# Delta rule heads in two overlapping lanes, one merge gate column behind each head, 14 merge gate columns ahead of the attention

## The chip, the cores and the metric

The kernel runs on one core of one Trainium2 chip. The metric is the device time of one execution in microseconds (us), median of several runs. A profile of one execution stands beside it: for every engine the instructions with their start and duration, what they waited for, and the clock that was granted to TensorE. PE is TensorE, DVE is VectorE, ACT is ScalarE, POOL is GpSimd, SP is SyncE, which issues the DMAs.

## The reference

One layer of a hybrid encoder for 512 prompt tokens and 8 x 16 decode tokens, 640 rows in all, in float32. Cut to what matters here:

```python
z = x @ w_in                     # 640 x 2048 by 2048 x 12312
q_a, k_a, v_a, f_a, gate_a, qkv_b, a_b, beta_b, gate_b, m_a, m_b = jnp.split(z, SPLIT_IDX, axis=-1)
# branch A: forgetting attention, 8 heads of 128
y_a = (o_a * jax.nn.silu(gate_a)) @ w_out_fox
# branch B: causal conv of width 4 on q|k|v, silu, l2 norm of q and k, then per head in chunks
u = solve(amat, vc * bc[..., None])
w = solve(amat, kb * jnp.exp(gc)[..., None])
def step(s, xs):
    v_new = u_n - w_n @ s
    o = q_n @ s + qk_n @ v_new
    s = s * gl_n + kt_n.T @ v_new
y_b = (rms_norm(o_b, gdn_norm_w) * jax.nn.silu(gate_b)) @ w_out_gdn
# merge: m_a and m_b are 2048 columns of z each, the merge gates
h = (jax.nn.sigmoid(m_a) * y_a + jax.nn.sigmoid(m_b) * y_b) @ w_out
# then layer norm, a gate projection and the per-layer embedding
```

## The kernel before

All large products are cut into **columns**: 128 output channels, 16 k-steps of 128 input channels, all 640 rows in two halves of 320. Each operand is split into a high and a low fp32r part, and three products are summed, so a k-step is six matmuls of 320 (`mm6`, L218 and L219) and a column is 96. There are 146 columns of weights, and TensorE works through them in a fixed order.

Weights come as half columns of 512 KB (`wr`, three buffers, issued by SyncE), and are split in pieces of 128 x 512 by ScalarE (`wh`, L167) and VectorE (`wl`, L168), up to six pieces ahead of their use (a column uses four).

The order around the columns is written out in Python. Each k-step ends with `tick()`, which lets each **lane** (a queue of generators) take one step when its time has come. What a generator issues between two `yield`s lands on the engines' queues at that k-step; `yield n` means n k-steps later. All engines take their instructions in the order written. So the small products of the heads stand between column matmuls, at places that the counts of `yield` set.

Stages: attention (`phase_fox`, 8 heads of q, k and gate columns, with the values' columns, L259, after the first q and k), the embedding's projection, the delta rule (`phase_gdn`), then the two output projections and the gate (`tail`). Merge gate columns (`mcol`) fill the stages in between: 3 behind the attention, 3 behind each of the delta rule's heads 0 to 6, 8 behind head 7.

A delta rule head is four columns (q, k, v and the output gate). After each of the first three, ScalarE writes the result to `strip` (L584), and the lane `conv` runs the convolution on VectorE: a first tap (L599) and three more (L603), a tanh on ScalarE, then L610 and L615. The lane `work` runs `gdn` and behind it `gdn_pro` and `gdn_dec`:

- transposes and squares (L630 to L645), norms and coefficients `cs` on VectorE (L664 to L676), transposed values (L686), key and query products (L699) with `lt` and `qk` (L706, L708);
- the unit triangular blocks of `lt` go through memory into `lanes`, and 31 steps of forward substitution run on VectorE (L732, L734); the result goes to memory (`xd`, L740) and comes back as `u0` (L743), and VectorE transposes it (L835);
- `gdn_pro`: TensorE reads that transposed tile first at L844, builds the larger inverse (L852 to L873), and then goes through the four chunks: L885 (with the state S), L891, L896, then VectorE's new state (L899, L901), L905 and L906. Each of these steps stands two k-steps behind the one that it needs;
- `gdn_dec`: the same for the decode rows with 8 states `st` (L793 to L826).

The lane `ends` runs `gdn_out` (norm and gate of the head's output, L759 to L779). A head waits to start until the output of the head before last is done. All head products share the PSUM tag "s" with four banks.

Of the kernel before, what the change touches and what calls it, by code (L numbers as in the profile page):

```python
# [17 lines left out]
P = 128  # L18
DM = 2048
T = 640  # L20
NPT = 512
# [25 lines left out]
class Kernel:  # L47
# [4 lines left out]

    PIECES = 6
    LATE = 3

# [563 lines left out]
    def gdn(self, h, kq, v, sg):  # L619
        nc, cb = self.nc, self.cb  # L620
        gr = self.zt([P, T], "gr")
        nc.sync.dma_start(out=gr, in_=bcast(self.rd[8 + h], T, P))
        st = self.zt([P, 8, P], "st")
        nc.sync.dma_start(out=st, in_=self.i["st"][h])

# [21 lines left out]
        dt = self.zt([P, 5, P], "dt")  # L647
        for t in range(5):
            m = C_DP if t < 4 else C_DD
# [26 lines left out]
        nc.vector.tensor_single_scalar(cs[:, 4, :], r[:, 5:10], GDN_SCALE, op=ALU.mult)  # L676
        kt = self.zt([P, 5, P], "kt")
        vr = self.zt([P, 5, P], "vr")
        for t in range(4):
# [11 lines left out]
        lt = self.zt([P, 5, P], "lt")  # L691
        qk = self.zt([P, 5, P], "qk")
        for t0 in (0, 2, 4):
# [18 lines left out]
        for a in range(4):  # L712
# [8 lines left out]
        for src, pad in ((kq[:, 0, NPT:T], self.kpad), (qg[:, NPT:T], self.gpad)):  # L721
            for par in range(2):
                nc.gpsimd.tensor_copy(
                    out=pad.rearrange("p (j two) c -> p j two c", two=2)[:, :, par, 16 * par:16 * par + 16],
                    in_=src.rearrange("p (j two c) -> p j two c", two=2, c=16)[:, :, par, :])
        yield 5
        x = self.zt([80, 8, 32], "sx", 2)
        tmp = self.zt([80, 8, 32], "sx2")
# [15 lines left out]
        yield 8  # L744
        uu = self.uu
        dd = [slice(32 * a, 32 * a + 32) for a in range(4)]
        for a in range(4):
            nc.gpsimd.tensor_copy(out=uu[dd[a], :, dd[a]], in_=u0[dd[a], :, :])
        yield from self.par(self.gdn_pro(h, kq, lt, qk, qg, kt, vr, cs, u0),
                            self.gdn_dec(h, qk, kt, vr, cs, st))  # L750
        self.ends["gens"].append(self.gdn_out(h, self.ob, cs, sg))

    def gdn_out(self, h, ob, cs, sg):

        nc = self.nc
# [12 lines left out]
        for t in range(5):  # L768
            nc.scalar.mul(ob[:, t, :], ob[:, t, :], f[:, t:t + 1])
        yield (30 if h < 7 else 3)  # L770
        og = self.zt([P, T], "og")
        po = self.sps()
        for t in range(4):
            nc.tensor.transpose(po[:, t * P:(t + 1) * P], ob[:, t, :], self.ident)
        nc.vector.scalar_tensor_tensor(out=og[:, 0:NPT], in0=po, scalar=self.nw, in1=sg[:, 0:NPT],
                                       op0=ALU.mult, op1=ALU.mult)
        po = self.sps()
        nc.tensor.transpose(po[:, 0:P], ob[:, 4, :], self.ident)
        nc.vector.scalar_tensor_tensor(out=og[:, NPT:T], in0=po[:, 0:P], scalar=self.nw, in1=sg[:, NPT:T],  # L779
                                       op0=ALU.mult, op1=ALU.mult)  # L780
        yield 2
        nc.sync.dma_start(out=self.ogd[8 + h], in_=og)
        self.gdone = h
        yield

    def gdn_dec(self, h, qk, kt, vr, cs, st):

        nc, cb = self.nc, self.cb
        self.ob = ob = self.zt([P, 5, P], "ob")
        pd = self.sps()  # L790
        for par in range(2):
# [11 lines left out]

        vm = self.zt([P, 2, P], "dt", 1, "vm")
        nc.gpsimd.tensor_tensor(out=vm, in0=vn[:, None, :].to_broadcast([P, 2, P]),
# [25 lines left out]
    def gdn_pro(self, h, kq, lt, qk, qg, kt, vr, cs, u0):  # L831
# [10 lines left out]
        for t in range(4):  # L842
            for a in (0, 64):
                nc.tensor.matmul(px[a + 32:a + 64, 32 * t:32 * t + 32], lt[a:a + 32, t, a + 32:a + 64],  # L844
                                 m0[a:a + 32, t, :], start=True, stop=True)
        xx = self.zt([P, 4, 32], "xx")
        for a in (32, 96):
# [18 lines left out]
        for t in range(4):  # L866
            nc.tensor.matmul(px[64:128, t * 64:(t + 1) * 64], lt[0:64, t, 64:128], t1[:, t, :], start=True, stop=True)
        x2 = self.zt([P, 4, 64], "x2")
        nc.scalar.copy(out=x2[64:128].rearrange("p a b -> p (a b)"), in_=px[64:128, 0:256])
# [44 lines left out]
    def run(self, ctx):  # L914
# [31 lines left out]
    def phase_fox(self, work):  # L946
# [71 lines left out]
        for h in range(H):  # L1018
# [3 lines left out]
            for c in range(3):  # L1022
# [51 lines left out]
    def phase_gdn(self, conv, work):  # L1074
# [7 lines left out]
        for x in (self.uu, self.t1, self.kpad, self.gpad):  # L1082
            nc.gpsimd.memset(x, 0.0)
        self.gdone = -1
        for h in range(H):
            self.until(lambda: self.gdone >= h - 2)
            kq = self.zt([P, 2, T], "kq", 2)
            v, sg = self.zt([P, T], "v"), self.zt([P, T], "sg", 2)
            for c in range(4):
                acc = self.column()[0]  # L1090
                self.until(lambda: not conv["gens"])
                if c == 3:
                    self.silu_evac(acc, sg, "cth")
                else:
                    ct = 8 * c + h
                    stp = self.strip_evac(acc, ct)
                    conv["gens"].append(self.conv_silu(stp, ct, (kq[:, 1, :], kq[:, 0, :], v)[c]))
# [315 lines left out]
def _layout(a):  # L1413
# [13 lines left out]
          for g in range(2)]  # L1427
    bl += [bq[0], bk[0], *bv[0], *bv[1], bg[0]]
    for h in range(1, H):
        bl += [bq[h], bk[h], bg[h]]  # L1430
    bl += m[:3]
    pj = _wblock(a["w_pl_proj"][0])
    pj = [pj[8 * i:8 * i + 8].transpose(1, 0, 2).reshape(P, DM) for i in range(2)]
    bl += [pj[0], pj[1]]
    for h in range(H):
        bl += [gq[h], gk[h], gv[h], gg[h]]
        if h < 7:
            bl += m[3 + 3 * h:6 + 3 * h]
    bl += m[24:]
    bl += list(_wblock(np.concatenate([a["w_out_fox"][0], a["w_out_gdn"][0]], 0)))  # L1440
# [68 lines left out]
```

## Time and profile before

| | |
|---|---|
| median of 3 runs | 2295.9 us (2295.38 to 2296.25) |
| profiled execution, its own time | 2294.97 us |
| its span, first to last instruction | 2293.1 us |
| mean granted TensorE clock | 0.999 |
| TensorE busy | 2285.8 us |
| VectorE busy | 1178.1 us |
| ScalarE busy | 727.7 us |
| HBM | 237.70 MB read, 40.67 MB written |

Matmuls are pipelined and their ends are modelled, so a busy TensorE says only that it had work in flight; how fast it goes is read from the starts of matmuls that follow each other. Rows of the order of time read: start, duration, engine, line, operation, written tile <- read tiles, shapes, count, and in brackets the idle time ahead and what ended it. A stage row reads: stretch, its length, then each engine's busy time with its count of instructions, the TensorE clock, the DMA share and GB/s.

### The profile page before, as it was taken

The numbers are of one execution on the slowest core, as the hardware profiler recorded it, in microseconds if no ns is written. First come the engines' busy times: TensorE is split into PE (matmuls) and PEld (weight loads), VectorE is DVE, ScalarE is ACT, GpSimd is POOL, SyncE is SP. The second block draws the span as 40 slices with busy tenths as digits, with TensorE's granted clock in tenths as the row PEclk, the third lists the DMA queues.
The fourth block names the chain that finished last, engine by engine and source line by source line (L and its number), as shares of the span: only waits on it lengthen the run. The fifth ranks groups of instructions, "written<-read, shape, count | busy, mean of one in ns | idle before, by whom it ended". The sixth has DMA issues, their size and how long they took to land.

```text
span 2293.1 us, 39837 instructions
## 1 busy us (share of the span) xinstructions
PE 2285.8 (100%) x16274; PEld 2202.9 (96%) x16274; DVE 1178.1 (51%) x2589; ACT 727.7 (32%) x1656; POOL 68.4 (3%) x230
## 2 busy tenths in 40 slices
PE   9999999999999999999999999999999999999999
PEld 7889999999999999999999999999999999999998
DVE  5224334433546565656565656554433533657555
ACT  4222223332523434242434242424111311333222
POOL 0000000000000000000000000000000000020000
PEclk9999999999999999999999999999999999999999
DMA  6345455444522322323232323235433322223331
GB/s 225 123 151 214 157 172 170 165 163 138 187 97 91 98 93 98 100 89 107 81 107 81 107 81 107 82 113 194 139 126 126 115 97 97 97 97 114 120 120 59
DMA packets 107431, 280.96 MB, mean 123 GB/s; under 512 B 21464, under 2 KB 28712, under 8 KB 107248
## 3 DMA queue, kind: packets, MB, share of 16 engines
q1 hardware_dynamic: 107248, 278.41, 36.2%
q8 instruction: 128, 2.10, 0.4%
q14 instruction: 55, 0.45, 0.1%
HBM read 237.70 MB, written 40.67 MB: 121 GB/s over the span
## 4 chain that ended last, share of the span: by engine, by line
PE 99%; DMA 0%; DVE 0%; SPq 0%; ACT 0%; issue 0%
PE g L218 43%; PE g L219 42%; PE g L259 4%; PE o L259 1%; PE s L511 1%; PE o L562 1%; PE s L471 1%; PE s L699 1%; PE s L821 0%; PE s L557 0%; PE s L906 0%; PE s L891 0%; PE s L896 0%; DMA wr<-in_w 0%; PE s L905 0%; PE s L885 0%
## 5 line engine op out<-in xcount | busy, mean ns | idle before, releaser
L168 DVE TENSOR_TENSOR wl<-wr,wh 128x512 fp32r<-128x512 f32 x584 | 400.4, 690 | 700.3 <-ACT wh L167 699.4
L218 PE MATMUL g<-xh,wh 128*128 128x320 f32 (+1 forms) x2160 | 694.7, 322 | 0.0
L218 PE MATMUL g<-xl,wh 128*128 128x320 f32 (+1 forms) x2160 | 668.5, 310 | 0.5 <-DVE xl L193 0.5
L219 PE MATMUL g<-xh,wh 128*128 128x320 f32 x2160 | 668.4, 309 | 0.0
L219 PE MATMUL g<-xl,wh 128*128 128x320 f32 x2160 | 668.2, 309 | 0.0
L219 PE MATMUL g<-xh,wl 128*128 128x320 f32 x2160 | 667.6, 309 | 0.0
L218 PE MATMUL g<-xh,wl 128*128 128x320 f32 (+1 forms) x2160 | 667.4, 309 | 0.0
L167 ACT CAST wh<-wr 128x512 fp32r<-128x512 f32 x584 | 361.0, 622 | 897.3 <-PE g L219 770.9
L218 PEld LDWEIGHTS g<-xh,wh 128*128 128x128 f32 x2160 | 407.1, 188 | 15.9 <-issue 13.4
L219 PEld LDWEIGHTS g<-xh,wh 128*128 128x128 f32 x2160 | 407.5, 189 | 0.8
L218 PEld LDWEIGHTS g<-xl,wh 128*128 128x128 f32 x2160 | 407.1, 188 | 1.0 <-DVE xl L193 1.0
L219 PEld LDWEIGHTS g<-xl,wh 128*128 128x128 f32 x2160 | 407.1, 188 | 0.0
L219 PEld LDWEIGHTS g<-xh,wl 128*128 128x128 f32 x2160 | 406.4, 188 | 0.0
L218 PEld LDWEIGHTS g<-xh,wl 128*128 128x128 f32 x2160 | 406.1, 188 | 0.1
L734 DVE TENSOR_TENSOR sx<-sx,sx 80x240 f32<-80x240 f32 (+14 forms) x240 | 68.2, 284 | 8.2
L732 DVE TENSOR_TENSOR sx<-sx,lanes 80x240 f32<-80x240 f32 (+14 forms) x240 | 68.2, 284 | 7.4
L603 DVE SCALAR_TENSOR_TENSOR cy<-strip,taps,cy 128x664 f32<-128x664 f32 x72 | 65.4, 909 | 2.1
L1224 DVE SCALAR_TENSOR_TENSOR sab<-sab,g 128x320 f32<-128x320 f32 x64 | 28.4, 485 | 69.4 <-PE g L218 64.2
L259 PE MATMUL g<-wh,xh 128*128 128x512 f32 x128 | 50.7, 396 | 0.0
L259 PE MATMUL g<-wl,xh 128*128 128x512 f32 x128 | 50.6, 395 | 0.0
L259 PE MATMUL g<-wh,xl 128*128 128x512 f32 x128 | 50.5, 394 | 0.0
L1070 ACT ACTIVATE m<-g 128x320 f32<-128x320 f32 x64 | 24.5, 435 | 67.5 <-PE g L218 67.5
(338 smaller groups left out, 1840.5 us busy)
## 6 DMA issues: line engine op xcount, KB each, us to landing
wr<-in_w SPq DMA_DIRECT2D x290, 512.0 KB
kc<-in_kc SPq DMA_DIRECT2D x32, 512.0 KB
vc<-in_vc SPq DMA_DIRECT2D x32, 512.0 KB
xr<-in_xT SPq DMA_DIRECT2D x32, 320.0 KB
md<-m SPq DMA_DIRECT2D x32, 320.0 KB
sab<-md SPq DMA_DIRECT2D x32, 320.0 KB
ogd<-og SPq DMA_DIRECT2D x16, 320.0 KB
ed<-e SPq DMA_DIRECT2D x16, 320.0 KB
```

The source lines that it names most:

```text
L167: nc.scalar.copy(out=hi, in_=src)
L168: nc.vector.tensor_tensor(out=lo, in0=src, in1=hi.bitcast(F32), op=ALU.subtract)
L218: nc.tensor.matmul(ps[0], whl[w], xhl[o][:, a], start=(first and x == 0), stop=(last and x == 2))
L219: nc.tensor.matmul(ps[1], whl[w], xhl[o][:, b], start=(first and x == 0), stop=(last and x == 2))
L259: nc.tensor.matmul(ps, x[:, sl], w, start=(s == 0 and n == 0), stop=(s == 15 and n == 2))
L471: nc.tensor.matmul(s1[32 * j:32 * j + 32, :], self.qpad[:, 2 * j + par, :], kc[:, (j % 2) * NPT:(j % 2 + 1) * NPT], start=(par == 0), stop ...
L511: nc.tensor.matmul(od[32 * j:32 * j + 32, 0:P], self.ppad[:, c, 2 * j + par, :], vc[:, o:o + P], start=False, stop=(par == 1 and c == 3), ...
L603: nc.vector.scalar_tensor_tensor(out=y[:, 0:CV], in0=strip[:, i:i + CV], scalar=tp[:, 4 * ct + i:4 * ct + i + 1], in1=y[:, 0:CV], op0=ALU. ...
L732: nc.vector.tensor_tensor(out=tmp[:, :, 0:n], in0=xo[:, :, j:j + 1].to_broadcast([80, 8, n]), in1=lanes[:, j:j + 1, j + 1:32].to_broadcast ...
L734: nc.vector.tensor_tensor(out=x[:, :, j + 1:32], in0=xo[:, :, j + 1:32], in1=tmp[:, :, 0:n], op=ALU.subtract)
L1070: nc.scalar.activation(m[:, hf * HALF:(hf + 1) * HALF], acc[hf], AF.Tanh, scale=0.5)
L1224: nc.vector.scalar_tensor_tensor(out=x[:, sl], in0=x[:, sl], scalar=1.0, in1=ps[hf], op0=ALU.add, op1=ALU.mult)
```

## The change

A head of the delta rule is cut in two. `gdn` ends when `u0` has been asked for, and hands the rest to a new generator, `gdn_chunks`, in a lane of its own (`self.chunks`). So the first part of head h + 1 runs beside the chunks of head h. Tiles that both need get second buffers (gr, kt, vr, qk), others share or lose one (lanes, sx, m0, sx2); the load of `st` and the padded copies move to the start of `gdn_chunks`, `gdn_dec` starts six k-steps later, and `gdn_out` waits 10 k-steps instead of 30 ahead of its transposes.

Gate columns: 14 stand behind the first q and k columns (`FRONT`), ahead of the values; 3 behind the attention as before; one (`FILL`) behind each of heads 0 to 6; 8 behind head 7 as before. The weights are laid out in the new order.

```diff
+    FRONT = 32 - 11 - 7
+    FILL = 1
@@ gdn
-        gr = self.zt([P, T], "gr")
+        gr = self.zt([P, T], "gr", 2)
-        st = self.zt([P, 8, P], "st")
-        nc.sync.dma_start(out=st, in_=self.i["st"][h])
-        kt = self.zt([P, 5, P], "kt")
-        vr = self.zt([P, 5, P], "vr")
+        kt = self.zt([P, 5, P], "kt", 2)
+        vr = self.zt([P, 5, P], "vr", 2)
-        qk = self.zt([P, 5, P], "qk")
+        qk = self.zt([P, 5, P], "qk", 2)
-        lanes = self.zt([80, 32, 32], "lv", 1, "lanes")
+        lanes = self.zt([80, 32, 32], "hl", 1, "lanes")
-        x = self.zt([80, 8, 32], "sx", 2)
+        x = self.zt([80, 8, 32], "sx")
         u0 = self.zt([P, 5, 32], "u0")
         nc.sync.dma_start(out=u0, in_=bass.AP(self.xd.tensor, self.xd.offset, [[32, P], [4096, 5], [1, 32]]))
         yield 8
-        uu = self.uu
+        self.chunks["gens"].append(self.gdn_chunks(h, kq, lt, qk, qg, kt, vr, cs, u0, sg))
+
+    def gdn_chunks(self, h, kq, lt, qk, qg, kt, vr, cs, u0, sg):
+        nc, uu = self.nc, self.uu
+        st = self.zt([P, 8, P], "st")
+        nc.sync.dma_start(out=st, in_=self.i["st"][h])
...
         for a in range(4):
             nc.gpsimd.tensor_copy(out=uu[dd[a], :, dd[a]], in_=u0[dd[a], :, :])
         yield from self.par(self.gdn_pro(h, kq, lt, qk, qg, kt, vr, cs, u0),
                             self.gdn_dec(h, qk, kt, vr, cs, st))
+        self.bdone = h
         self.ends["gens"].append(self.gdn_out(h, self.ob, cs, sg))
@@ gdn_out
-        yield (30 if h < 7 else 3)
-        og = self.zt([P, T], "og")
+        yield (10 if h < 7 else 3)
+        og = sg
@@ gdn_dec
         self.ob = ob = self.zt([P, 5, P], "ob")
+        yield 6
@@ run
+        self.chunks = self.lane()
@@ phase_fox
                     if h == 0:
+                        for _ in range(self.FRONT):
+                            self.mcol("sc")
                         values(0)
                         values(1)
@@ phase_gdn
         for h in range(H):
-            self.until(lambda: self.gdone >= h - 2)
-            kq = self.zt([P, 2, T], "kq", 2)
-            v, sg = self.zt([P, T], "v"), self.zt([P, T], "sg", 2)
             for c in range(4):
                 acc = self.column()[0]
+                if c == 0:
+                    self.until(lambda: self.bdone >= h - 2)
+                    kq = self.zt([P, 2, T], "kq", 2)
+                if c == 2:
+                    v = self.zt([P, T], "v")
                 self.until(lambda: not conv["gens"])
                 if c == 3:
+                    self.until(lambda: self.gdone >= h - 2)
+                    sg = self.zt([P, T], "sg", 2)
                     self.silu_evac(acc, sg, "cth")
...
-            for _ in range(3 if h < 7 else 6):
+            for _ in range(self.FILL if h < 7 else 6):
                 self.mcol("cth")
```

How this moves instructions, at the places of which the prediction speaks. Lines of the changed kernel are 2 to 8 higher than before behind the additions: L899 is the former L891, L904 L896, L909 L901, L727 and L729 the substitution's L732 and L734.

VectorE in the delta rule, the end of a head's norms, before (`cs` holds the coefficients, `wl` is a weight piece, `hl` the next split of keys and queries):

```order
L674 TENSOR_TENSOR cs<-rry,ecol 128x5
L675 TENSOR_TENSOR cs<-cs,rry 128x5
L676 TENSOR_SCALAR cs<-rry 128x5
L168 TENSOR_TENSOR wl<-wr,wh 128x512 x2
L664 TENSOR_TENSOR hl<-kq,hl 128x512
```

And now (`S` is the state of the head before, `rp` the right side of its next chunk):

```order
L674 TENSOR_TENSOR cs<-rry,ecol 128x5
L675 TENSOR_TENSOR cs<-cs,rry 128x5
L676 TENSOR_SCALAR cs<-rry 128x5
L909 SCALAR_TENSOR_TENSOR S<-S,gl,s 128x128
L895 SCALAR_TENSOR_TENSOR rp<-s,negc,vr 128x128
L170 TENSOR_TENSOR wl<-wr,wh 128x512
```

The state update of one head now stands behind the norms of the next.

TensorE at the same place now, without the column matmuls between (two k-steps lie between L899 and L904, one between L914 and L686, and one between L686 and L893):

```order
L899 MATMUL s<-rp,uu 128x128
...
L904 MATMUL s<-vn,kt 128x128
L913 MATMUL s<-S,gr 128x128
L914 MATMUL s<-vn,qk 128x128
...
L686 MATMUL s<-cb,v 128x128 x4
...
L893 MATMUL s<-S,kq 128x128
```

Before, nothing of another head stood near L686; now the transposes of one head (L686) stand between the chunk steps of the other, and L893 reads the S of the VectorE row above.

VectorE at the end of a substitution, before (`sx` is the solution, `lanes` the blocks, `m` the transposed result):

```order
L732 TENSOR_TENSOR sx_8553<-sx,lanes 80x8
L734 TENSOR_TENSOR sx<-sx,sx_8553 80x8
L168 TENSOR_TENSOR wl<-wr,wh 128x512 x4
L835 STREAM_TRANSPOSE m_8843<-u_8771 128x128
```

And now:

```order
L601 TENSOR_SCALAR cy<-strip,taps 128x664
...
L605 SCALAR_TENSOR_TENSOR cy<-strip,taps,cy 128x664
L727 TENSOR_TENSOR sx_13145<-sx,lanes 80x8
L729 TENSOR_TENSOR sx<-sx,sx_13145 80x8
L605 SCALAR_TENSOR_TENSOR cy<-strip,taps,cy 128x664
L170 TENSOR_TENSOR wl<-wr,wh 128x512
L612 SCALAR_TENSOR_TENSOR kq<-cth,cy 128x512
L617 SCALAR_TENSOR_TENSOR kq<-cth,cy 128x128
L170 TENSOR_TENSOR wl<-wr,wh 128x512 x3
L601 TENSOR_SCALAR cy<-strip,taps 128x664
L843 STREAM_TRANSPOSE m_13461<-u_13378 128x128
```

The next head's convolutions (`cy`) now stand inside the substitution and between it and the transposition; earlier in it stand L612 and L617 of the convolution before.

More of the change, by code (lines that the diff above doesn't have):

```diff
@@ L717, in gdn @@
         yield 5
-        lanes = self.zt([80, 32, 32], "lv", 1, "lanes")
+        lanes = self.zt([80, 32, 32], "hl", 1, "lanes")
         nc.sync.dma_start(out=lanes.rearrange("p j i -> p (j i)"),
                           in_=bass.AP(self.ld.tensor, self.ld.offset, [[1024, 20], [0, 4], [1, 1024]]))
[L721 to L725, printed above, removed]
         yield 5
-        x = self.zt([80, 8, 32], "sx", 2)
+        x = self.zt([80, 8, 32], "sx")
         tmp = self.zt([80, 8, 32], "sx2")
@@ L744, in gdn @@
         yield 8
-        uu = self.uu
+        self.chunks["gens"].append(self.gdn_chunks(h, kq, lt, qk, qg, kt, vr, cs, u0, sg))
[3 more added lines that the diff above has]
+        nc.sync.dma_start(out=st, in_=self.i["st"][h])
+        for src, pad in ((kq[:, 0, NPT:T], self.kpad), (qg[:, NPT:T], self.gpad)):
+            for par in range(2):
+                nc.gpsimd.tensor_copy(
+                    out=pad.rearrange("p (j two) c -> p j two c", two=2)[:, :, par, 16 * par:16 * par + 16],
+                    in_=src.rearrange("p (j two c) -> p j two c", two=2, c=16)[:, :, par, :])
         dd = [slice(32 * a, 32 * a + 32) for a in range(4)]
@@ L802, in gdn_dec @@
         nc.scalar.mul(vn, pd[:, 0:P], cs[:, 2, 4:5])
-        vm = self.zt([P, 2, P], "dt", 1, "vm")
+        vm = self.zt([P, 2, P], "vm")
         nc.gpsimd.tensor_tensor(out=vm, in0=vn[:, None, :].to_broadcast([P, 2, P]),
@@ L845, in gdn_pro @@
                                  m0[a:a + 32, t, :], start=True, stop=True)
-        xx = self.zt([P, 4, 32], "xx")
+        xx = self.zt([P, 4, 32], "m0", 1, "xx")
         for a in (32, 96):
@@ L867, in gdn_pro @@
             nc.tensor.matmul(px[64:128, t * 64:(t + 1) * 64], lt[0:64, t, 64:128], t1[:, t, :], start=True, stop=True)
-        x2 = self.zt([P, 4, 64], "x2")
+        x2 = self.zt([P, 4, 64], "sx2", 1, "x2")
         nc.scalar.copy(out=x2[64:128].rearrange("p a b -> p (a b)"), in_=px[64:128, 0:256])
@@ L1427, in _layout @@
           for g in range(2)]
-    bl += [bq[0], bk[0], *bv[0], *bv[1], bg[0]]
+    nf, r = Kernel.FRONT, Kernel.FILL
+    bl += [bq[0], bk[0], *m[:nf], *bv[0], *bv[1], bg[0]]
     for h in range(1, H):
         bl += [bq[h], bk[h], bg[h]]
-    bl += m[:3]
+    bl += m[nf:nf + 3]
     pj = _wblock(a["w_pl_proj"][0])
@@ L1437, in _layout @@
         if h < 7:
-            bl += m[3 + 3 * h:6 + 3 * h]
-    bl += m[24:]
+            bl += m[nf + 3 + r * h:nf + 3 + r * (h + 1)]
+    bl += m[nf + 3 + 7 * r:]
     bl += list(_wblock(np.concatenate([a["w_out_fox"][0], a["w_out_gdn"][0]], 0)))
```

4 lines of the change are left out of this document (2 added, 2 removed).

## The prediction

> **What bounds the kernel now.** I read the page first (busy shares, then the chain that ended last), then the engines' busy time by stage, then the spacing of single matmuls in the order of time.
>
> ```profile
> span 2293.1 us, 39837 instructions
> PE 2285.8 (100%) x16274; PEld 2202.9 (96%) x16274; DVE 1178.1 (51%) x2589; ACT 727.7 (32%) x1656; POOL 68.4 (3%) x230
> PE 99%; DMA 0%; DVE 0%; SPq 0%; ACT 0%; issue 0%
> 900.00:1100.00 200.00, 200.00 (x1506) 195.04 (x1505) 123.44 (x348) 72.94 (x206) 10.47 (x34) 1.00 0.31 99
> 1101.37 0.31 PE L218 MATMUL g<-xh,wl 128*128 128x320 f32 x1
> 1101.51 0.31 PE L219 MATMUL g<-xh,wl 128*128 128x320 f32 x1
> 1101.66 0.39 PE L891 MATMUL s<-vr,uu 128*128 128x128 f32 x2
> 1101.80 0.39 PE L218 MATMUL g<-xh,wh 128*128 128x320 f32 x1
> 1102.03 0.31 PE L219 MATMUL g<-xh,wh 128*128 128x320 f32 x1
> ```
>
> TensorE is busy for the whole span, at the full granted clock (the 1.00 in the stage row), and the chain that ended last is 99% TensorE. In the stage 900 to 1100, in the middle of the delta rule, VectorE has 123.4 of 200 us. The single rows say what a busy TensorE is here: column matmuls start 0.147 us apart, and two fp32 passes of a head (L891) put between them take 1102.03 - 1101.51 - 2 x 0.147 = 0.23 us, which is what they would take anywhere. So the kernel is a list of TensorE work with no holes. Moving work on that list cannot shorten it; it can only open holes. Where a TensorE instruction has to wait, every column matmul behind it waits too, and the end moves by as much. The question is which waits the new order makes.
>
> **The change part by part.** The columns are the same 146, and each head has the same products. What is cheap first. The 14 gate columns ahead of the values cost what they cost elsewhere. In the list of TensorE's order the groups of head work between columns fall from 351 to 338; by the rows above a break costs nothing beyond its passes, at most the 0.23 us of a small group, so the 13 are worth 0 to 3 us, and I take 1. Second buffers (gr, kt, vr, qk) free no wait that the trace shows. The state load (st) is now issued at the start of the chunks, six k-steps (5.3 us) ahead of its first reader; I take 0 for it, since the hole that I find below stands between the two, and a load that is late all the same would only lengthen that hole.
>
> The price is the cover. The seven-column heads gave 112 k-steps each (a k-step is six column matmuls, 0.88 us); five columns give 80. Two in-order engines, VectorE above all, now run two heads' steps at once at places where TensorE waits for them.
>
> *Wait B, the substitution.* The chain in a head of the kernel before (head 1):
>
> ```profile
> 829.64 0.77 ACT L1070 ACTIVATE m<-g 128x320 f32<-128x320 f32 x2 [3.10 <-PE g L218]
> 834.23 0.40 DVE L732 TENSOR_TENSOR sx<-eye,lanes 80x248 f32<-80x248 f32 x1
> 855.81 0.17 DVE L734 TENSOR_TENSOR sx<-sx,sx 80x8 f32<-80x8 f32 x1
> 856.01 0.34 SPq L740 DMA_DIRECT2D xd<-sx  x1
> 857.73 0.38 SPq L743 DMA_DIRECT2D u<-xd  x1
> 859.85 0.31 DVE L835 STREAM_TRANSPOSE m<-u 128x128 f32<-128x128 f32 x1
> 861.21 0.44 PE L844 MATMUL s<-m,lt 32*32 32x32 f32 x16
> L844 PE MATMUL s<-m,lt x128: 190/191/213, 748.5 to 1537.9; 32*32 32x32 f32 x128
> ```
>
> The substitution fills VectorE from 834.23, 4.6 us after the end of a column (829.64), to 855.98. Its result goes out and back through memory, is transposed at 860.16, and TensorE reads it at 861.21. Only 1.05 us are spare; with the signal's way I count 1.0. In the list of the changed order the reader stands as far behind the last L699 as before (258 column matmuls both times), but the lane columns of the next head are now q and k columns instead of gate columns, so VectorE gets convolutions just there:
>
> ```profile
> 878.96 0.43 ACT L584 COPY strip<-g 128x320 f32<-128x320 f32 x1
> 880.93 0.56 DVE L599 TENSOR_SCALAR cy<-strip,taps 128x664 f32<-128x664 f32 x1
> 881.67 2.79 DVE L603 SCALAR_TENSOR_TENSOR cy<-strip,taps,cy 128x664 f32<-128x664 f32 x3
> 885.35 0.69 DVE L610 SCALAR_TENSOR_TENSOR kq<-cth,cy 128x512 f32<-128x512 f32 x1
> 885.96 0.29 DVE L615 SCALAR_TENSOR_TENSOR kq<-cth,cy 128x128 f32<-128x128 f32 x1
> 821.35 0.75 DVE L775 SCALAR_TENSOR_TENSOR og<-s,cvec,sg 128x512 f32<-128x512 f32 x1 [2.02 <-PE s L774]
> 822.01 0.34 DVE L779 SCALAR_TENSOR_TENSOR og<-s,cvec,sg 128x128 f32<-128x128 f32 x1
> 855.92 1.90 DVE L168 TENSOR_TENSOR wl<-wr,wh 128x512 fp32r<-128x512 f32 x3
> ```
>
> - Ahead of the substitution: a convolution's taps end 881.67 + 2.79 - 878.96 = 5.5 us after their column; then the last head's output products (822.35 - 821.35 = 1.0) and one weight piece (1.90 / 3 = 0.6) make 7.1 instead of 4.6: +2.5 us.
> - Inside it, by the changed order: the rest of that convolution (0.9) and of the next one the first tap (0.5) and two more (2 x 0.93): +3.2 us.
> - Behind it, ahead of the transposition: one tap, a weight piece, the convolution's end after a tanh, three weight pieces and the next first tap, 0.9 + 0.6 + 0.9 + 1.9 + 0.5 = 4.8 and about 1.1 for ScalarE in between, so 5.9 instead of the 4.2 of the way through memory (855.98 to 860.16): +1.7 us.
>
> So 2.5 + 3.2 + 1.7 - 1.0 = 6.4 us of TensorE idle in a head. Bounds: 3.7 (1.5 ahead, nothing behind) and 8 (another 1.6 of ScalarE). Heads 1 to 6 have it, head 0 without the output products (5.4), head 7 has gate columns behind it and none: 6 x 6.4 + 5.4 = 44 us.
>
> *Wait A, the state behind the norms.*
>
> ```profile
> 803.56 0.73 ACT L655 ACTIVATE gr<-gr 128x640 f32<-128x640 f32 x1
> 804.70 0.62 ACT L663 CAST hl<-kq 128x512 fp32r<-128x512 f32 x1
> 804.74 0.60 PE L686 MATMUL s<-cb,v 128*128 128x128 f32 x4
> 805.44 0.68 DVE L664 TENSOR_TENSOR hl<-kq,hl 128x512 fp32r<-128x512 f32 x1
> 808.93 0.17 DVE L676 TENSOR_SCALAR cs<-rry 128x5 f32<-128x5 f32 x1
> 884.98 0.34 DVE L901 SCALAR_TENSOR_TENSOR S<-S,gl,s 128x128 f32<-128x128 f32 x1
> 801.47 0.28 ACT L645 ACTIVATE junk<-s 128x128 f32<-128x128 f32 x1 [0.23 <-PE s L643]
> ```
>
> VectorE's norms and coefficients (L664 to L676) run to 809.10, 4.36 us after TensorE has passed L686; before, nothing on TensorE waited for them. In the changed order the previous head's state update L901 stands right behind them on VectorE, and TensorE needs that state two places on (the next L885, and by a shared PSUM bank already L686): 4.36 + 0.34 = 4.7 us. TensorE gets there later, by the nine products of the other lane between (9 x 0.23 = 2.1); the norms start later too, since their last squares wait for TensorE (the 0.23 at 801.47) and ScalarE has two more instructions ahead: +1.4. That leaves 4.0 us, with bounds of 2.6 (norms not delayed) and 5. Seven heads: 28 us. The four PSUM banks also make one state product wait for a VectorE read once in a head, 0.34 and the way there: 0.5 x 7 = 3.5 us.
>
> *The clock after a wait.*
>
> ```profile
> 2288.00:2293.00 5.00, 0.00 (x0) 0.00 (x0) 1.29 (x4) 0.51 (x1) 0.00 (x0) 0.74 0.08 26
> 2287.21 0.28 PE L212 MATMUL g<-xh,wl 128*128 128x256 f32 x1
> 1.19 4.02 PE L969 MATMUL wu<-z 128*128 128x512 bf16 x9 [1.19 <-DVE z L966]
> 5.69 0.47 PE L218 MATMUL g<-xl,wh 128*128 128x320 f32 x1
> 5.95 0.47 PE L219 MATMUL g<-xl,wh 128*128 128x320 f32 x1
> 7.05 0.30 PE L219 MATMUL g<-xh,wh 128*128 128x320 f32 x1
> ```
>
> The last matmul ends at 2287.49; a mean clock of 0.74 over the next 5 us, if it goes from 1 to the 0.5 of the slow rows, puts the drop 2.9 us after it. At the start the pace is 0.267 us (5.69 to 5.95) until about 7, 5.9 us after the first matmul. A hole as long as B closes the clock, then; one costs up to 5.9 x (1 - 0.147 / 0.267) = 2.65 us, at least 0. I take 2.0, near the upper end since 6.4 is well past 2.9: 7 x 2.0 = 14 us. For A (4.0) I take none.
>
> The Trainium skill, "TensorE: Matmul & The Clock Gate", Part 1, says that the clock is halved after a whole idle window of about 3.4 us of a free-running counter. By that, as an estimate, a hole of 6.4 us holds a window 9 times in 10 and one of 4.0 about 2 times in 10, so the term would be some 7 x 2.65 x 1.1 = 20 us. The single drop at 2.9 us here is no contradiction that a trace of before can settle.
>
> **Sum**: 44 + 28 + 3.5 + 14 - 1 = 88 us. The profiled execution took 2294.97 us (span 2293.1), 0.9 below the median of the three runs; 2295 + 88 = 2383.
>
> **Rivals.**
> 1. One of the two waits never reaches TensorE. For: each rests on a few us between queues, and the norms may start earlier than I think. A alone gives 2295 + 28 + 3.5 = 2326; B alone 2295 + 44 + 14 = 2353.
> 2. The clock closes at A too. For: 4.0 is past 2.9. Against: 2.9 is one drop, and 4.0 is not far past it. 2383 + 7 x 2.65 + 7 x 0.65 = 2406. By the Trainium skill's window, as an estimate, B closes it and A seldom does, which gives 2389.
> 3. Not slower: VectorE takes the convolutions in its own gaps. In this stage 38% of its time is free, and ahead of head 1's substitution it sat idle 1.98 us for a weight piece. If that gap and the pieces of lead let the substitution end within 1.0 us of its present place, B is nothing, and if ScalarE reaches the norms 4 us earlier, A is nothing: 2293 to 2296. Against: the order puts 3.2 us inside the substitution, where it has no gap. This decides at 1.0 us.
> 4. Faster: the 13 breaks, 3 us; inside 0.2%.
>
> **How the numbers follow.** The forecast with both waits and the clock at B has 0.47, rival 1 0.24, rival 2 0.17, rivals 3 and 4 0.09, and something later still (weight loads behind a blocked SyncE) 0.03. Predicted 2383. The range goes from A alone at its lower bound (2295 + 7 x 2.6 = 2313, so 2314) to both at their upper bounds with some clock (2295 + 7 x 13.5 + 32 = 2421): 2314 to 2421. A measurement here tells 0.2%, 4.6 us, from no change: faster 0.02, same 0.08, slower 0.90.
>
> **What would show it.** The first reader of the transposed tile came every 112.8 us before ((1537.9 - 748.5) / 7). Two columns fewer are 2 x 96 x 0.147 = 28.2 us, so without waits 84.6; I expect 97. Waits of TensorE on the transposition of about 6.4 us, seven, none for head 7; waits on the state update of about 4, seven; slices with a granted clock under 1 from 750 us on, and none in the attention. The attention and the tail should take what they took. A reader spaced 85 us would refute both waits; large waits of TensorE on weight pieces would mean a cause that I have not counted.

## The result, and the profile after

The changed kernel takes 2391.95 us (median of 4 runs, 2387.70 to 2393.19) where the kernel before took 2295.98 on the same chip: 1.0415 times as long, 95% interval 1.0397 to 1.0433. Its profiled execution has a span of 2389.7 us, 96.6 more than the 2293.1 of before.

The page of the changed kernel (span, busy times, chain that ended last by engine, granted clock in 40 slices):

```profile
span 2389.7 us, 39829 instructions
PE 2322.5 (97%) x16274; PEld 2230.4 (93%) x16274; DVE 1177.2 (49%) x2589; ACT 728.4 (30%) x1656; POOL 83.2 (3%) x230
PEclk9999999999999999999899998999999999999999
PE 87%; DVE 8%; ACT 2%; issue 1%; DMA 1%; SPq 0%; ACTq 0%
```

The work is the same: 16274 matmuls, and VectorE is busy for 1177 us (1178 before). But TensorE's share of the chain has gone from 99% to 87%, VectorE's from 0% to 8%. The holes are in one stage. The stage rows of the changed kernel, attention and then 100 us of the delta rule:

```profile
200.00:870.00 670.00, 670.00 (x4694) 617.59 (x4693) 247.42 (x477) 198.09 (x431) 6.95 (x28) 1.00 0.45 154
...
1000.00:1100.00 100.00, 91.51 (x660) 87.76 (x658) 63.31 (x183) 34.59 (x102) 7.97 (x21) 0.93 0.25 84
```

In the attention TensorE is busy for all 670 us at full clock. In the delta rule it stands still for 8.5 us of 100 and the granted clock falls to 0.93. What it waits for, from the view of waits (us in total, times, longest):

```profile
PE s L852 <- DVE m L843: 34.0, 7, 5.2
PE s L686 <- DVE S L909: 22.6, 7, 3.2
```

These are the two waits of the forecast, seven times each. (A third and much shorter one is priced in the balance below.) In head 1, TensorE's rows in the order of time show what the first one costs:

```profile
1042.73 0.31 PE L221 MATMUL g<-xh,wl 128*128 128x320 f32 x1
1047.93 0.64 PE L852 MATMUL s<-m,lt 32*32 32x32 f32 x16 [4.89 <-DVE m L843]
...
1048.93 0.47 PE L221 MATMUL g<-xh,wh 128*128 128x320 f32 x1
1049.20 0.47 PE L220 MATMUL g<-xl,wh 128*128 128x320 f32 x1
```

From 1042.73 to 1047.93 are 5.20 us between two starts that should be 0.147 apart: a hole of 5.05. And when work comes back, column matmuls start 0.27 us apart (1048.93, 1049.20) instead of 0.147. Summed over the seven heads the holes ahead of L852 are 35.2 us and those ahead of L686 23.8.

What VectorE did meanwhile, its rows from the substitution's last step (L729) to the transposition (L843):

```profile
1042.30 0.17 DVE L729 TENSOR_TENSOR sx<-sx,sx 80x8 f32<-80x8 f32 x1
1042.39 0.90 DVE L605 SCALAR_TENSOR_TENSOR cy<-strip,taps,cy 128x664 f32<-128x664 f32 x1
1043.21 0.68 DVE L170 TENSOR_TENSOR wl<-wr,wh 128x512 fp32r<-128x512 f32 x1
1044.17 0.69 DVE L612 SCALAR_TENSOR_TENSOR kq<-cth,cy 128x512 f32<-128x512 f32 x1 [0.28 <-ACT cth L610]
...
1046.43 0.75 DVE L170 TENSOR_TENSOR wl<-wr,wh 128x512 fp32r<-128x512 f32 x1 [0.16 <-ACT wh L169]
...
1047.58 0.30 DVE L843 STREAM_TRANSPOSE m<-u 128x128 f32<-128x128 f32 x1
```

In the rows left out are two more weight pieces, the end of one convolution and the first tap of the next. An engine that is 49% busy over the span has 0.28 + 0.16 us of idle time in these 5.3: it works on the next head while TensorE waits for the 0.30 us at the bottom.

The second wait, near 1180, rows of VectorE and TensorE (part of the norms left out):

```profile
1176.61 0.69 DVE L664 TENSOR_TENSOR hl<-kq,hl 128x512 fp32r<-128x512 f32 x1
...
1180.10 0.17 DVE L676 TENSOR_SCALAR cs<-rry 128x5 f32<-128x5 f32 x1
1180.17 0.34 DVE L909 SCALAR_TENSOR_TENSOR S<-S,gl,s 128x128 f32<-128x128 f32 x1
...
1175.51 0.49 PE L904 MATMUL s<-vn,kt 128*128 128x128 f32 x2 [0.36 <-ACT vn L901]
1177.02 0.31 PE L221 MATMUL g<-xh,wl 128*128 128x320 f32 x1
1180.56 1.12 PE L686 MATMUL s<-cb,v 128*128 128x128 f32 x4 [3.23 <-DVE S L909]
```

The state product (L904) was done on TensorE at 1176.0, and its update L909 could have run then. It stands behind eighteen instructions of the other head (L664 to L676) and runs at 1180.17. L686 itself doesn't read `S`: it writes to a PSUM bank, and the bank is free only when L909 has read L904's product out of it. The first reader of `S`, L893, stands one k-step behind L686. So one more bank would, as an estimate from these rows, still leave a wait of some 2 us there (1180.56 less 1177.17, where L686 was due, 0.44 for its four products and 0.88 for the k-step); this wasn't tested.

**The balance** of the 96.6 us: 35.2 and 23.8 for the two waits; 0.66 in a head for a group that waits for a PSUM bank, 4.6 in all (1.36 us against 0.70 for the same four products where nothing holds them, in the rows below; the wait is for L895, whose tile `rp` they don't read); 0.63 in a head for L904, 4.4 in all, since the step that makes its `vn` (L901) stands on ScalarE behind the other head's squares and exponentials (L645 to L655) and starts at 1175.11, 1.7 us after the product that it needs (the 0.36 at L904 above is the idle part of it); and some 29 left, which the slow clock must account for. The experiments measure it by itself.

```profile
1164.51 0.70 PE L829 MATMUL s<-vm,kt 32*128 32x256 f32 x4
...
1169.40 1.36 PE L829 MATMUL s<-vm,kt 32*128 32x256 f32 x4
1170.07 0.29 PEld L829 LDWEIGHTS s<-vm,kt 32*128 32x128 f32 x2 [0.37 <-DVE rp L895]
```

### The profile page after: what moved, and what is told of

Its sections match the earlier page's. It is cut to its first block, busy times and chain, and to the rows that moved or that the text cites. A ratio compares the mean times of both kernels' runs of the same rounds, so it can differ in the third digit from the quotient of the medians.

```text
span 2389.7 us, 39829 instructions
## 1 busy us (share of the span) xinstructions
PE 2322.5 (97%) x16274; PEld 2230.4 (93%) x16274; DVE 1177.2 (49%) x2589; ACT 728.4 (30%) x1656; POOL 83.2 (3%) x230
## 4 chain that ended last, share of the span: by engine, by line
PE 87%; DVE 8%; ACT 2%; issue 1%; DMA 1%; SPq 0%; ACTq 0%
PE g L220 37%; PE g L221 36%; PE g L261 4%; DVE sx L727 2%; DVE sx L729 2%; DMA wr<-in_w 1%; DVE wl L170 1%; PE o L261 1%; ACT wh L169 1%; PE s L513 1%; DVE cy L605 1%; PE o L564 1%; PE s L473 1%; PE s L829 1%; PE s L699 1%
## 5 line engine op out<-in xcount | busy, mean ns | idle before, releaser
L729 DVE TENSOR_TENSOR sx<-sx,sx 80x240 f32<-80x240 f32 (+14 forms) x240 | 68.3, 285 | 8.2
L727 DVE TENSOR_TENSOR sx<-sx,lanes 80x240 f32<-80x240 f32 (+14 forms) x240 | 68.3, 284 | 6.5
L610 ACT ACTIVATE cth<-cy 128x664 f32<-128x664 f32 x24 | 18.2, 759 | 106.9 <-DVE cy L605 106.8
```

Source lines behind the costliest of these rows:

```text
L727: nc.vector.tensor_tensor(out=tmp[:, :, 0:n], in0=xo[:, :, j:j + 1].to_broadcast([80, 8, n]), in1=lanes[:, j:j + 1, j + 1:32].to_broadcast ...
L729: nc.vector.tensor_tensor(out=x[:, :, j + 1:32], in0=xo[:, :, j + 1:32], in1=tmp[:, :, 0:n], op=ALU.subtract)
```

## The experiments

The theory: two steps of VectorE's in-order queue stand behind the other head's work, and TensorE waits for each once in a head; every hole also slows the clock for a while. The rivals: something other than the queue makes the tiles late (the way through memory, ScalarE, PSUM banks); the lanes themselves cost the time, not the missing columns; the slow clock is free.

### The 14 columns back between the heads

```diff
-    FRONT = 32 - 11 - 7
-    FILL = 1
+    FRONT = 32 - 11 - 21
+    FILL = 3
```

> Two lanes and all buffers as in the changed kernel, but three gate columns behind each head again and none ahead of the attention. Theory (the cost is two heads' VectorE work meeting where TensorE waits, plus the clock after it): with 112 k-steps a head the chunks end before the next head's norms, and gate columns stand beside the substitution, so both waits and all slow-clock stretches vanish: 2294 to 2300 us. Rival (the lane split itself, the later state load or the shared buffers cost): above 2340 us.

Measured: 2303.34 us (2302.98 to 2304.76), 1.0035 times the kernel before (1.0022 to 1.0048). The clock is 1.00 throughout, and no matmul of a head is held for more than 0.4 us. The stage row of this kernel:

```profile
1100.00:1300.00 200.00, 199.00 (x1453) 194.46 (x1453) 115.19 (x310) 73.14 (x208) 10.21 (x32) 1.00 0.27 92
```

So the two lanes alone cost 7.8 us, 3 more than the bracket allowed; the other 88 of the 96 come with the columns that were taken out of the stage. The 7.8 are small waits: the group at L785 takes 4.4 us more over the eight heads, the one at L852 2.1.

### Half of them back

```diff
+    FRONT = 32 - 11 - 14
+    FILL = 2
```

> Two lanes, two gate columns behind each head, seven ahead of the attention. Theory: the wait on the state behind the norms is gone (the orders no longer meet there); at the substitution one convolution instead of one and a half stands in the way, about 3 us a head in place of 5, and holes of 3 us close the clock in some heads: 2317 to 2336 us. Rival (cost in proportion to the gate columns moved): half of the 96 us, 2344 us.

Measured: 2354.58 us, 1.0255 (1.0240 to 1.0270). The wait ahead of L852 fell to 2.6 us as expected, the one behind the norms is gone, and a new one is there that nobody had priced. The waits of this kernel:

```profile
PE s L852 <- DVE m L843: 18.1, 7, 3.2
PE s L699 <- ACT hl L663: 16.5, 7, 2.4
```

And its rows around one of the new ones, ScalarE and TensorE:

```profile
1223.03 1.57 ACT L776 ACTIVATE ob<-ob,rfy 128x128 f32<-128x128 f32 x5 [1.52 <-DVE rfy L773]
1224.51 0.60 ACT L169 CAST wh<-wr 128x512 fp32r<-128x512 f32 x1
1225.02 0.61 ACT L663 CAST hl<-kq 128x512 fp32r<-128x512 f32 x1
1225.68 0.58 PE L699 MATMUL s<-hl 128*128 128x256 f32 x1 [2.36 <-ACT hl L663]
```

ScalarE stands still for 1.52 us at L776, because that step of the head before wants a norm that VectorE is still making. Behind it waits L663, which the other lane needs now. The time is 19 us over its bracket and 11 over the rival's 2344: another spacing of the same lanes makes other steps collide.

### The convolutions shortened

The last three of the four taps of each convolution are left out:

```diff
-            nc.vector.scalar_tensor_tensor(out=y[:, 0:CV], in0=strip[:, i:i + CV],
-                                           scalar=tp[:, 4 * ct + i:4 * ct + i + 1], in1=y[:, 0:CV],
-                                           op0=ALU.mult, op1=ALU.add)
```

> The changed kernel without the last three taps of each convolution (L605); the convolution then has its first tap alone, and VectorE has 2.8 us less per convolution, about as much ahead of, inside and behind the substitution. Theory (the wait on the transposed tile is VectorE's queue: two lanes' steps in one order): that wait falls from 5.2 us to 0 to 1.5 in each of the seven heads, the slow stretches of the clock behind it (44 us in all) go, the wait on the state behind the norms stays at 3.2 and its slow stretches too: 2392 - 7 x 4.2 - 20 = 2343, between 2335 and 2352. Rival (the way through memory or ScalarE sets the transposed tile's time): the wait stays over 4 us and the time over 2380.

Measured: 2354.87 us, 1.0251 (1.0236 to 1.0266), 37 less than the changed kernel. Waits of this kernel:

```profile
PE s L683 <- DVE S L906: 22.7, 7, 3.2
...
PE s L849 <- DVE m L840: 9.4, 8, 2.4
```

The wait on the transposed tile went from 4.9 to 1.2 us; the other stayed at 3.2. So it is VectorE's queue. The time is 3 us over the expected bracket. The waits there lost 24.6 us in the view (34.0 to 9.4), not the 29 taken; and the slow stretches behind this wait did go (44 us to 7), but they are worth less than the 20 us taken for them, as the fills below show.

### The norms shortened

The three Newton steps of the reciprocal square root are left out of the norms of keys and queries:

```diff
-    def rsqrt(self, x, n, name):
+    def rsqrt(self, x, n, name, steps=3):
...
-        for _ in range(3):
+        for _ in range(steps):
...
-        r = self.rsqrt(ss, 10, "rr")
+        r = self.rsqrt(ss, 10, "rr", 0)
```

> The changed kernel without the three Newton steps in the norms of keys and queries (nine small VectorE instructions of 0.2 us between L664 and L676 in each head), so the norms end 1.85 us earlier. Theory (the state update stands behind the norms on VectorE, and TensorE waits for it): the wait at L686 falls from 3.2 to about 1.4 in seven heads, 13 us, and the clock closes there less often (up to 15 us more): 2365 to 2380. The wait on the transposed tile stays at 5.2. Rival (the wait at L686 is ruled by something other than the norms, a PSUM bank or ScalarE): it stays over 3 us and the time within 5 us of 2392.

Measured: 2367.17 us, 1.0310 (1.0293 to 1.0327), inside the bracket. Waits of this kernel:

```profile
PE s L686 <- DVE S L909: 9.8, 7, 1.4
```

Nine instructions less on VectorE, 1.85 us, and TensorE's wait is 1.8 us shorter (3.2 to 1.4). The state update is late by VectorE's queue, to the us.

### The norms earlier

In the changed kernel VectorE stood idle for 3.27 us just ahead of L664, until ScalarE, behind two exponentials (L654, L655), had made its half of a weight piece. Now the exponentials go behind the coefficients, and `pieces(0, True)` leaves the low part of the split to a later place:

```diff
-        yield
-        nc.scalar.activation(dt, dt, AF.Exp)
-        nc.scalar.activation(gr, gr, AF.Exp)
-        yield
+        yield 2
...
-        hl = pieces(0)
+        hl = pieces(0, True)
...
         nc.scalar.mul(vr[:, 4, :], pd[:, P:2 * P], cs[:, 0, 4:5])
+        nc.scalar.activation(dt, dt, AF.Exp)
+        nc.scalar.activation(gr, gr, AF.Exp)
         yield 2
+        nc.vector.tensor_tensor(out=hl[1], in0=kq[:, :, 0:2 * P], in1=hl[0].bitcast(F32), op=ALU.subtract)
```

> The changed kernel with the head's norms issued ahead of the exponentials and of the low part of the key split, so that VectorE reaches the other head's state update some 3 us earlier. Theory: the seven waits of TensorE at L686 (3.4 us each, 24 us) shrink to under 0.5 us, and the slow-clock stretches that start there go (34 us of them at half clock, 15 us): 2350 to 2360 us, waits on the transposition unchanged at 5 us. Rival (the wait only moves to the next chunk step, whose right side stands behind the same work): 2380 to 2392 us.

Measured: 2371.67 us, 1.0331 (1.0316 to 1.0347): 20 less, where 32 to 42 were expected. The waits, and VectorE's and ScalarE's rows ahead of the norms (L665) in this kernel:

```profile
PE s L687 <- DVE S L910: 14.1, 7, 2.0
```

```profile
1167.86 0.36 ACT L902 ACTIVATE vn<-s,cs 128x128 f32<-128x128 f32 x1
...
1168.77 0.69 DVE L170 TENSOR_TENSOR wl<-wr,wh 128x512 fp32r<-128x512 f32 x1 [2.03 <-ACT wh L169]
1169.38 0.16 DVE L665 TENSOR_SCALAR ss<-ss 128x10 f32<-128x10 f32 x1
```

VectorE was free for 2.03 us, but next in its order stood a weight piece whose other half ScalarE made only at 1168.12, behind the head's own squares (L645, until 1167.97) and a step of the other head (L902). The norms were moved past the exponentials, not past this piece. They need those squares too, so without it they could have started at about 1168.0 instead of 1169.38, and, by that estimate, 0.6 of the 2.0 us would have stayed. The wait of the state product on `vn` is gone, as the exponentials no longer stand ahead of that step: its group takes 0.67 us again, where it took 1.30.

### The reader later

```diff
-        yield 8
+        yield 15
```

> The changed kernel with the start of the chunks seven k-steps (6.2 us) later, nothing else. Theory: the wait on the transposition (5.0 us, seven times, 35 us) and the slow-clock stretches behind it (44 us at half clock, 20 us) vanish, the wait on the state stays but lies at another chunk step, 1 to 3.5 us: 2325 to 2345 us. Rival (VectorE has too much work in 80 k-steps, so a later reader finds the queue as late as before): above 2375 us.

Measured: 2389.74 us, 1.0409 (1.0391 to 1.0426): no better, as the rival had it. The waits, and VectorE's rows ahead of the transposition:

```profile
PE s L829 <- DVE st L834: 28.6, 7, 4.3
PE s L852 <- DVE m L843: 25.3, 7, 3.7
```

```profile
1047.53 2.82 DVE L605 SCALAR_TENSOR_TENSOR cy<-strip,taps,cy 128x664 f32<-128x664 f32 x3
...
1051.84 0.29 DVE L617 SCALAR_TENSOR_TENSOR v<-cth,cy 128x128 f32<-128x128 f32 x1
1052.05 0.30 DVE L843 STREAM_TRANSPOSE m<-u 128x128 f32<-128x128 f32 x1
```

The count in `yield` sets both the reader's place on TensorE and the transposition's place on VectorE. Seven k-steps later, three more taps and a convolution's end stand ahead of it: it runs at 1052.05 instead of 1047.58 (head 1). TensorE comes to the reader 5.7 us later (1048.5 instead of 1042.9), its tile 4.5 later. The other wait now ends with the update of the decode states (`st`) and is longer than that on `S` was. L829 doesn't read `st`, so this too is a wait for a PSUM bank, which that update must first read.

### Both queues relieved

Three of the edits above at once: norms ahead, no Newton steps, no last three taps.

> The norms ahead of the exponentials and of the keys' low part, no Newton steps, and no last three taps, all at once. Theory (the two waits and the clock behind them are the whole loss): the wait at the state update falls from 2.0 to about 0.2, the one on the transposed tile to 0 to 1.5, and with no hole of 2 us left the clock stays open: 2296 plus 7 x 0.2, 7 x 1 and 4.6 for the products that wait for a PSUM bank, 2298 to 2315. Rival (a third cause, such as weight pieces that come late or fewer columns to cover the heads): over 2325 with small waits at both places.

Measured: 2315.29 us, 1.0083 (1.0068 to 1.0098), 0.3 over the bracket. The view lists two waits of TensorE on the heads' tiles, 0.2 us each time at the state update (L684, seven times), and this one:

```profile
PE s L850 <- DVE m L841: 7.9, 7, 2.6
```

One slow stretch of 3.4 us is left in the delta rule. So no third large cause is left.

### The holes filled, to price the clock

Matmuls whose results nobody uses, put inside the waits, leave the waited-for tiles as late as before, and keep TensorE busy.

```diff
+        if h < 7:
+            z = self.ident.bitcast(BF16)
+            for _ in range(40):
+                nc.tensor.matmul(px[:, 0:256], z[:, 0:P], z, start=True, stop=True)
```

> The changed kernel with 40 more matmuls (bf16, 128 x 256, about 0.11 us each at full clock, 4.3 us together; results are not used) ahead of the products that read the transposed tile, in heads 0 to 6, so that they lie inside the wait. Theory (part of the loss is the clock that closes after a hole and stays at half for 3.4 or 6.8 us): the wait is filled, the transposed tile comes no later, and the slow stretches behind it, 44 us in all at about 0.55 of the pace, go: 2392 - 20 = 2372, between 2366 and 2378. Rival (the slow stretches cost nothing because the next wait takes them up, or the added matmuls only add their own time): 2390 or more.

Measured: 2376.00 us, 1.0348 (1.0333 to 1.0364). TensorE's rows of this kernel in head 1:

```profile
1042.68 4.54 PE L853 MATMUL s<-cb 128*128 128x256 bf16 x40
1047.63 0.44 PE L856 MATMUL s<-m,lt 32*32 32x32 f32 x16 [0.41 <-DVE m L843]
```

The reader starts 4.95 us after the fill began, where it started 5.05 into the hole, so the wait is as long as it was (within 0.1 us); but the 44.4 us of slow stretches behind it are gone, and 16 us of time with them. That is the price of the clock there, at 0.36 us for each us at half clock.

The second wait was filled too, first with 28 such matmuls ahead of L686, into the bank of the keys' squares (`pq`):

> As fill_wait, with 28 more such matmuls (3.0 us) ahead of the transposes at L686 in heads 1 to 7, so that they lie inside the wait on the state update as well. Theory (the clock goes to half at a fixed grid of 3.41 us when some 2 us of the 3.41 before were idle): with both waits filled no slow stretch is left in the delta rule; the 31 us of them that stood behind the second wait in fill_wait cost 0.45 each: 2376 - 14 = 2362, between 2357 and 2367. What is left over the kernel before is then the two waits themselves, 35 + 24, and the bank waits. Rival (the slow stretches follow from something else than the idle time, such as the load of the chip): as many slow stretches as before, and 2376 or more.

Measured: 2411.04 us, 1.0504 (1.0487 to 1.0522): slower than any other. The wait of this kernel:

```profile
PE s L921 <- DVE S L917: 31.9, 7, 4.6
```

The wait had moved a k-step ahead of the fill, to L921. That product reads the old state, not the new one, so it cannot wait for the update's result: what it takes is the PSUM bank that the update must still read. The fill had held one of the four banks until then. So this run doesn't price the clock, but it shows how short the lanes are of banks. The kernel with the earlier norms, with 40 and 18 matmuls at the same two places, fared alike: expected at 2338 to 2350 us, it took 2390.18, 1.0411 (1.0395 to 1.0426), and its wait too had moved ahead of the fill (L922, 3.3 us, seven times). The next one puts the fill in the bank of L921 itself, which is free at that place:

```diff
             po = self.sps()
+            if t == 1 and h < 7:
+                z = self.ident.bitcast(BF16)
+                for _ in range(28):
+                    nc.tensor.matmul(po[:, 256:512], z[:, 0:P], z, start=True, stop=True)
```

> As fill_wait, with 28 more such matmuls (3.0 us) in the second chunk of heads 0 to 6, behind the state product and ahead of the output product, into a PSUM bank that is free there. So no bank is held longer than in the changed kernel (in fill_both one was), and the fill lies one k-step ahead of the wait at L686. Theory (the clock follows the idle time in a fixed grid of 3.41 us): the wait at L686 shrinks by the 3.0 us of the fill, and no slow stretch is left in the delta rule: 2376 - 14 = 2362, between 2356 and 2367. Rival (the wait moves ahead of the fill again, or the fill only adds its own time): a wait of over 2 us stays and the time is 2376 or more.

Measured: 2364.69 us, 1.0301 (1.0283 to 1.0318), as expected. Its stage row, and the wait at L686 that is left:

```profile
1100.00:1300.00 200.00, 197.66 (x1515) 188.79 (x1514) 132.07 (x369) 71.45 (x209) 16.48 (x46) 1.00 0.27 89
```

```profile
1170.00 0.66 PE L686 MATMUL s<-cb,v 128*128 128x128 f32 x4 [0.18 <-DVE S L913]
```

No slow stretch is left in the delta rule. With all waits as long as in the changed kernel, to 0.1 or 0.2 us each, the kernel is 2391.95 - 2364.69 = 27.3 us faster: that is what the clock cost in the change. The same two fills in the kernel with the earlier norms:

> norms_first with both fills (40 matmuls ahead of the products on the transposed tile, 18 in the second chunk as in fill_both_2). Theory: the 61 us of slow stretches of norms_first go at 0.45 each: 2372 - 28 = 2344, between 2338 and 2350; what is left over the kernel before is the two waits, 35 + 15, less what the fills miss. Rival (the clock's share is smaller): 2355 or more.

Measured: 2351.67 us, 1.0242 (1.0227 to 1.0257), 20.0 less than without the fills and 2 over the bracket: 0.33 us for each of the 61 us of slow stretches, not 0.45. It is the fastest form of the change with one column behind a head that computes the whole result, and still 56 us behind the kernel before. No version beats that one. What one head at a time with fewer columns between would do wasn't tried.

## Why the prediction was right

**Wait B, the substitution: right, each term a little large.** Forecast 44 us, measured 35.2. Distances in head 1, before and after: from the last L699 to the substitution's first step 11.86 and 14.07 us (+2.2; forecast +2.5); the substitution itself 21.75 and 24.03 (+2.3; forecast +3.2); from its end to the end of the transposition 4.18 and 5.40 (+1.2; forecast +1.7). The sum, 5.7, less the spare 1.0, is 4.7; TensorE came to the place 0.3 earlier, and the hole is 5.0. Head 0 has 4.7 (5.4 forecast), and head 7 none, as forecast. The shortened convolutions show that it is this queue.

**Wait A, the state behind the norms: right, 4.0 forecast, 3.4 measured, 23.8 in all.** Two corrections were both too large, and their errors of 0.6 and 1.15 us, in opposite ways, cancelled in part. TensorE reaches L686 5.48 us after L643 instead of 3.97, 1.5 later and not 2.1; and the norms end 8.58 us after L643 instead of 8.33, 0.25 later and not 1.4. So 4.36 + 0.34 + 0.25 - 1.5 = 3.45. The shortened norms show the mechanism. That the wait comes at L686, by the PSUM bank, is as the prediction had it.

**The bank wait:** 3.5 forecast, 4.6 measured.

**The clock: the one term that was mis-sized.** Forecast 14 us, measured by the fills 27.3. The step that failed is the sentence "For A (4.0) I take none": the clock closed behind the second wait in six of seven heads, though that wait was even shorter than forecast. This is rival 2's mechanism. Behind the first wait the price was 15.9 / 7 = 2.3 a head, against the 2.0 taken. The Trainium skill, "TensorE: Matmul & The Clock Gate", Part 1, names one idle window of about 3.4 us as what it takes; holes of 2.2 us closed the clock here (in the kernel with the earlier norms), so in this case the measurement decides.

The waits came out 13 us under the forecast and the clock 13 over it, so the sum of 88 against the measured 96 is nearer than its terms. That is luck. Of the 96.6 between the spans, 59.0 are the two waits, 4.6 the bank, 27.3 the clock, and 4.4 the wait on `vn` behind ScalarE's exponentials, a term that the sum doesn't have; 1.3 stay unassigned. Rivals 1, 3 and 4 are out, since both waits are there seven times each.

**What would show it.** The reader came every (1633.9 - 950.4) / 7 = 97.6 us (97 forecast, 84.6 without waits). The clock fell from 950 us on and never in the attention. (The 750 of the forecast leaves out that the 14 columns ahead of the attention move the stage by 14 x 96 x 0.147 = 198 us.) From the last head's reader to the end it took 755.2 us before and 755.8 after.

## What to carry to other kernels

On engines that take their work in order, overlapping two chains brings both into one queue: before moving a step, list what stands ahead of it on every engine at its new place, and how long that takes, since an engine that is half idle can still be the one that is late. Independent TensorE work that is spread between dependent steps is cover, and its worth is seen only when it is gone: here the lanes without their columns cost 96 us, and with them 8. A delay count that places both the producer and its consumer moves the two together, so here it bought no slack. And unused matmuls in a hole that can't be closed bought back 16 to 27 us of slow clock here, as long as the PSUM bank that they write was free.

## What the runs showed of the hardware

**The clock falls on a grid, and less than a whole idle window is enough.** In every run that has slow stretches in the delta rule, they are 3.41 or 6.83 us long there and begin on one grid of 3.41 us; in the changed kernel all thirteen. The stage rows of the changed kernel, cut along that grid around head 1's first wait (stretch, length, TensorE busy, its weight loads, VectorE, ScalarE, GpSimd, clock, DMA share, GB/s):

```profile
1042.78:1046.20 3.42, 0.26 (x2) 0.00 (x0) 3.14 (x6) 2.81 (x7) 0.97 (x3) 1.00 0.24 48
1046.20:1049.60 3.40, 1.67 (x20) 1.60 (x21) 3.20 (x6) 1.31 (x5) 3.36 (x8) 0.50 0.92 302
1049.60:1053.00 3.40, 3.40 (x35) 3.01 (x34) 1.92 (x5) 1.38 (x2) 1.81 (x3) 0.50 0.47 165
1053.00:1056.40 3.40, 3.40 (x38) 2.94 (x39) 1.68 (x5) 0.37 (x1) 0.00 (x0) 1.00 0.00 0
```

After an idle window the clock is halved for the next; that one was still half idle, and the clock stayed at half for another; then a busy one opened it. How idle a window must be is seen with shorter holes: one in the kernel with the earlier norms, one in that with the shorter norms, each cut along its own grid:

```profile
1073.57:1076.98 3.41, 1.46 (x12) 1.20 (x10) 2.97 (x20) 0.64 (x4) 0.00 (x0) 1.00 0.00 0
1076.98:1080.39 3.41, 3.34 (x14) 3.35 (x15) 0.77 (x3) 3.41 (x12) 0.00 (x0) 0.51 0.03 5
```

```profile
1075.19:1078.60 3.41, 2.01 (x17) 1.75 (x16) 2.54 (x11) 1.86 (x7) 0.00 (x0) 1.00 0.00 0
1078.60:1082.01 3.41, 3.41 (x27) 3.41 (x27) 1.04 (x2) 2.00 (x8) 0.00 (x0) 1.00 0.02 5
```

TensorE busy for 1.46 of 3.41 us: closed. For 2.01: open. Counting the idle time of a window from the starts of matmuls, in eight kernels and at full clock: of 71 windows after which the clock fell, 70 had 2.0 us or more of idle time and one 1.76; of some 100 with over 0.3 us after which it didn't, none had more than 2.06. So about 2 us of idle time in 3.41 decide here. Holes at the second wait of 1.56 us (the shorter norms) never closed the clock in 7, holes of 2.17 us (the earlier norms) did in 5 of 7, holes of 3.40 us (three kernels) in 20 of 21: a hole near 2 us closes it or not by where it falls on the grid.

**One PSUM bank held a little longer cost 46 us.** The two kernels with both waits filled have as many added matmuls, and differ in the bank that 28 of them write and, by one k-step, in their place: 2411.0 against 2364.7 us. In the slower one seven holes of 4.7 us stand open ahead of the fill, and 41.0 us of slow stretches follow them. The Trainium skill, "Perfetto Trace Analysis", Optimization Strategy, says that a gap which repeats can mean that tiles lack room in SBUF or PSUM; here the wait on `S` in that run's rows is one, though the name beside it is that of the state.
